# Where the lo half of a weight tile is computed: GpSimd subtraction, or ScalarE negation and an accumulating DMA

## Chip, core and metric

One core of a Trainium2 chip runs the whole kernel. The metric is the device time of one execution in microseconds; lower is better. The engines named here are TensorE (PE in the profile; its weight loads are PEld), VectorE (DVE), ScalarE (ACT), GpSimd (POOL) and SyncE (SP), which here only issues DMAs. A letter q behind an engine's name means its queue, not the engine's datapath.

## What is computed

One layer of a decoder trunk on 256 tokens of width 2048, in float32. Cut to what matters here:

```
x <- LN(alpha*x + 0.5*SwiGLU_1(x))
x <- LN(alpha*x + W_out concat[GatedDeltaNet | HGRN2 | S5 | RG-LRU](split(x W_in)))
x <- LN(alpha*x + 0.5*SwiGLU_2(x))
x <- LN(alpha*x + (p W_p) * sigmoid(x W_g))

swiglu(x, wi, wo):  gate, up = split(x @ wi);  (silu(gate) * up) @ wo      # 2048 -> 2 x 5632 -> 2048
layer_norm(x, g, b): (x - mean) * rsqrt(var + 1e-5) * g + b
```

The weights of the two SwiGLU blocks, of the mixer's two projections and of the embedding gate are read once each, 684 tiles of 128 x 1024 float32 in all.

## The kernel before

Every large product is made three times on float32r operands, so that it keeps float32 accuracy: x and the weights are each split into a high part (the value rounded to float32r) and a low part (the rest), and `mm3` (line 138) adds hi*hi, hi*lo and lo*hi into one PSUM bank.

The weights come as a stream of tiles in the order of use (`wq`). `load_w` (line 106) issues one load of 512 KB from SyncE's queue into a raw tile wr. `pump` (line 115) then makes two tiles from it: wh, by a cast on ScalarE (line 126), and wl = wr - wh, by a subtraction (line 128) on VectorE, or on GpSimd when `pool_mod` is set and the tile's number is a multiple of it. `get` (line 132) hands the next pair to the products and pumps the tiles behind it; `budget` says how many split and how many raw tiles are kept ahead (2 to 8 split ones).

All of wr, wh, wl, and also x, its transposed halves xh and xl, the hidden halves hh and hl, the gains g and biases b, live in one pool of 43 slots of 128 x 1024 words. A tile's slot goes to a later tile in program order, and the first writer of the later tile waits until the last reader of the earlier one is done. The schedule is manual: each engine runs its instructions in the order in which the program issues them.

`pool_mod` is 2 (every second lo tile on GpSimd) in the last six groups of a down projection, in the mixer, in the first of the eleven column blocks of the second SwiGLU and in the embedding's product up to its last group, 1 (every one) in the last group of a SwiGLU's down projection and of the mixer's output projection, from where it holds until the layer norm behind it is done, and 0 in the rest of the SwiGLU blocks.

At the end of such a projection (`down`, line 322; `out_proj`, line 1412) the first token half T=0 is finished before T=1. `evac` (line 163) adds the result to x and takes its statistics, and `ln_gen` (line 169) is a generator whose steps are put between the products of T=1 and those of the next block: a pow of one column on GpSimd (line 175), two steps of VectorE per quarter of x (lines 181 and 182), and `xt_piece` (line 231), which transposes a quarter on TensorE (line 236), casts it on ScalarE to xh (line 238) and subtracts on VectorE to xl (line 239). TensorE's instructions for it stand in the middle of the products. The four or five tiles of the next block that are split ahead are issued before these steps.

Of the kernel before, what the change touches and what calls it, by code (L numbers as in the profile page):

```python
# [20 lines left out]
LN_EPS = 1e-5  # L21
RMS_EPS = 1e-6
NSLOT = 43
RAMP = (0, 0, 1, 2, 4)  # weight tiles split ahead of the first products


class Build:
# [57 lines left out]
        self.cnt[key] = self.cnt.get(key, 0) + 1  # L85

    def tick(self, part=None):
        """one step of every running generator, or (part 0 or 1) of every other one."""
        for g in list(self.bg):
            if part is not None and self.side.setdefault(id(g), len(self.side) % 2) != part:  # L90
                continue
            try:
                next(g)
            except StopIteration:
                self.bg.remove(g)
                self.done.append(g)
# [3 lines left out]
            self.tick()  # L100

    def budget(self, split, raw):
        """weight tiles kept ready ahead of the products: split ones, and raw ones behind them."""
        self.n_split, self.n_raw = split, raw

    def load_w(self, n):
# [8 lines left out]
    def pump(self):  # L115
        nc = self.nc
        n = len(self.wq)
        es, ed = min(self.pg + self.n_split, n), min(self.pg + self.n_split + self.n_raw, n)
        while self.pd < ed or self.ps < es:
            if self.pd < ed:  # L120
                self.load_w(1)
            if self.ps < min(es, self.pd):
                r = self.raw.pop(self.ps)
                hi = self.slot((1024,), F32R, "wh")
                lo = self.slot((1024,), F32R, "wl")
                nc.scalar.copy(out=hi, in_=r)  # L126
                eng = nc.gpsimd if self.pool_mod and self.ps % self.pool_mod == 0 else nc.vector
                eng.tensor_tensor(out=lo, in0=r, in1=hi.bitcast(F32), op=ALU.subtract)  # L128
                self.hilo[self.ps] = (hi, lo)
                self.ps += 1  # L130

# [188 lines left out]
        self.down(KF, self.hT, [2], [4], i * 2)  # L320

    def down(self, K, lhs, first, last, li, final=False, evac=None):
        """x <- LN(alpha*x + lhs @ W), W streamed as [128, 2048] rows."""
        gs = self.groups(K, first, last)
        ps = [None, None]
        st = [self.work(24, "st") for _ in range(2)]
        k0 = 0
        gb = None
        for gi, gn in enumerate(gs):
            end = k0 + gn == K  # L330
            if gi == len(gs) - 10:
                gb = self.load_gb(li)
                self.budget(*((6, 2) if final else (8, 3)))
                if li == 0:
                    self.beta_dec()
            if gi == len(gs) - 6:
                self.pool_mod = 2
            if end:
                self.drain()
                if final:  # L340
                    self.pool_mod = 0
                else:
                    self.pool_mod = 1
                    self.budget(5, 2)
                    self.new_xt()
            wt = []
            for T in range(2):
                if k0 == 0:
                    if T:
                        self.drain() if K == KF else None  # L350
                    ps[T] = [self.bank() for _ in range(4)]
                if not end:
                    for kk in range(gn):
                        if T == 0:
                            wt += [self.get(), self.get()]
                        xhi, xlo = lhs(T, k0 + kk)
                        for n in range(4):
                            whi, wlo = wt[2 * kk + n // 2]
                            s = slice((n % 2) * 512, (n % 2) * 512 + 512)
                            self.mm3(ps[T][n], xhi, xlo, whi[:, s], wlo[:, s], k0 + kk == 0, False)  # L360
                        self.tick()
                else:
                    for n in range(4):
                        for kk in range(gn):
                            if T == 0 and n % 2 == 0:
                                wt.append(self.get())
                            xhi, xlo = lhs(T, k0 + kk)
                            whi, wlo = wt[kk + gn * (n // 2)]
                            s = slice((n % 2) * 512, (n % 2) * 512 + 512)
                            self.mm3(ps[T][n], xhi, xlo, whi[:, s], wlo[:, s], k0 + kk == 0, kk == gn - 1)  # L370
                            if kk == 1:
                                self.tick()
                        (evac or self.evac)(T, n, ps[T][n], st[T])
                        self.tick()
                    self.bg.append(self.ln_gen(T, st[T], gb, final))
                    self.tick()
            k0 += gn

# [1 line left out]
    def small(self, shape, name="m"):  # L380
        n = 1
        for d in shape:
# [25 lines left out]
        self.nc.scalar.activation(out=out, in_=a, func=f, **kw)  # L408

    def load_xt(self):  # L410
        """transposed x and the first weights, in the order in which they are used."""
        nc = self.nc
        self.new_xt()
        src = self.a["xT"].rearrange("(n c p) t -> p n c t", n=4, p=128)
# [32 lines left out]
            for h in range(2):  # L447
                self.nc.gpsimd.dma_start(out=self.x[T][h], in_=self.a["x"][0, T * 128:(T + 1) * 128, h * 1024:(h + 1) * 1024])

# [1 line left out]
    def load_params(self):  # L451
        nc, a = self.nc, self.a
        nc.gpsimd.dma_start(out=self.ident, in_=a["cst"][:, 0:128])
# [12 lines left out]
        return self.chp[:, i:i + 4]  # L466

    def softplus(self, x, n):
        """log(1 + e^x) = max(x, 0) + 2 atanh(e / (2 + e)), e = exp(-|x|), for small tiles."""
        W = lambda: self.small((n,), "sp")  # L470
        e, s, s2, q, mx = W(), W(), W(), W(), W()
        self.act(e, x, AF.Abs)
# [49 lines left out]
        self.act(self.eA, self.row[:, 0:4], AF.Exp)  # L522
        yield

# [1 line left out]
    def s5_prep(self):  # L526
        nc, a = self.nc, self.a
        S = lambda *sh: self.small(sh, "s5")
# [39 lines left out]
        yield  # L568

        def sincos(cs, sn, hs, m, n, ph):  # L570
            """cos, sin and sin^2(half) of m * (rh + rl); m, n, ph like cs."""
            sh = [128, cs.shape[1], 16] if cs.shape[2] == 16 else [128, 16, cs.shape[2]]
            if cs.shape[2] == 16:
                bh, bl = (v[:, None, :].to_broadcast(sh) for v in (rh, rl))
# [75 lines left out]
        Bre, Bim, Cre, Cim = (BC.rearrange("p (q g d) -> p q g d", q=4, g=16)[:, i] for i in range(4))  # L650

        def cmul(o_re, o_im, ar_, ai_, br_, bi_, q, neg_im=False):
            """complex product over the groups q; o_re and o_im get (rows, lhs, rhs, op) calls."""
            k = q.stop - q.start
            bc = lambda v: v[:, q, None].to_broadcast([128, k, 16])
            a1, a2 = u1[:, 0:k], u2[:, 0:k]
# [91 lines left out]
        return t  # L748

    def split_to(self, src, hi, lo):  # L750
        """src (f32, SBUF or PSUM) -> exact pair of float32r tiles."""
        self.nc.scalar.copy(out=hi, in_=src)
        self.sub(lo, src, hi.bitcast(F32))

    def rms_cm(self, y, gcol, key):
        """rms norm over 512 channels on the partitions, y [128, 4, 256] -> hi/lo."""
        nc = self.nc
        sq = self.slot((4, 256), F32, "sq")
        self.act(sq, y, AF.Square)
# [108 lines left out]
        yield  # L868
        yield from self.rms_cm(z, 84, "c")

# [1 line left out]
    def tail(self, o, T, key):  # L872
        """o [128 tokens, 4 heads, 128] in PSUM -> rms norm * gate, transposed into self.y[key]."""
        nc = self.nc
        sq = self.t2(4)
        ss = self.work(4, "ss", bufs=4)
# [21 lines left out]
        self.y[key] = (self.slot((4, 256), F32R, "yh"), self.slot((4, 256), F32R, "yl"))  # L898

    def gate_in(self, T, ps, gz, norm):  # L900
        """gz[:, T] = silu(ps) * norm gain (per head)."""
        z = gz[:, T].rearrange("p (a b) -> p a b", a=4)
        self.act(z, ps, AF.Silu)
        self.mul(z, z, norm[:, None, :].to_broadcast([128, 4, 128]), self.nc.gpsimd)

# [1 line left out]
    def hgrn_f(self, ps):  # L907
        F, K = self.slot((4, 256), F32, "F"), self.slot((4, 256), F32, "K")
        self.hF, self.hK = F, K
# [84 lines left out]
            yield  # L994
            yield

# [1 line left out]
    def conv(self, ps, acc, w, bias=None):  # L998
        nc = self.nc
        pad = self.W.tile([128, 4, 260], F32, tag="pad", name=self.nm("pad"))  # L1000
# [10 lines left out]
            if c % 2:  # L1011
                yield

# [1 line left out]
    def gdn_bd(self, ps):  # L1015
        """beta, decay logits -> per-token gates and the decay matrices."""
        nc = self.nc
        bd = self.slot((256,), F32, "bd")[0:16]
        nc.scalar.copy(out=bd, in_=ps)
# [42 lines left out]
        self.flags.add("D")  # L1062

    def tok(self, src, n):
        """token-major copy in PSUM of chunk n of channel-major src."""
        ps = self.bank((4, 128), "tok")
        for h in range(4):
            self.nc.tensor.transpose(ps[:, h], src[:, h, n * 128:(n + 1) * 128], self.ident)
# [13 lines left out]
        return ss[:, :, None].to_broadcast([128, 4, 128])  # L1082

    def tr_to(self, src, dst, neg=False):
        """dst <- per-head transpose of src [128, 4, 128]."""
        ps = self.bank((4, 128), "trt")
        for h in range(4):
            self.nc.tensor.transpose(ps[:, h], src[:, h], self.ident)  # L1088
# [64 lines left out]
        self.bg.append(self.gdn_inv(1))  # L1153

    def gdn_inv(self, n):
        """Q = transpose of (I + A)^-1, by doubling blocks along the diagonal."""
        nc = self.nc
        AT = self.AT[:, n]
        TQ = self.slot((2, 4, 128), F32, "TQ")
# [86 lines left out]
            nc.tensor.matmul(po[:, h], lhsT=self.qk[:, 1, h], rhs=uh[:, 1, h], start=False, stop=True)  # L1246
        yield from self.tail(po, 1, "a")

# [1 line left out]
    def lru_x(self, ps):  # L1250
        nc = self.nc
        wab = self.slot((8, 128), F32, "wab")
# [40 lines left out]
        yield  # L1293
        yield from self.rms_cm(y, 88, "d")

# [1 line left out]
    CHUNKS = (("t", 3080, "bi"), ("c", 4104, "cu"), ("c", 512, "ak"), ("c", 0, "aq"), ("c", 2568, "bf"), ("c", 1024, "av"),  # L1297
              ("c", 2056, "bq"), ("c", 4616, "dx"), ("c", 5128, "dg"), ("t", 3592, "bg"), ("t", 1536, "az"))
    ORDER = (("c", 1024), ("d", 1536), ("b", 512), ("a", 0))
# [155 lines left out]
    def busy(self, key):  # L1455
        return self.cnt.get(key, 0) < {"a": 2, "b": 2, "c": 1, "d": 1}[key]

# [1 line left out]
    def q_ple(self):  # L1459
        w, g = self.a["ple_w"][0], self.a["ple_gate_w"][0]  # L1460
        for half in range(2):
# [61 lines left out]


def _pack(inputs):
    """Layout of the inputs for the chip: transposed, concatenated, zero-padded; nothing is computed."""
    import numpy as np

    f = np.float32
# [67 lines left out]
```

## Time and profile before

| what | value |
|---|---|
| median of 3 runs | 2131.03 us (2126.71 to 2131.29) |
| span of the profiled execution | 2125.8 us; no separate time is given for it, the three runs lie 0.9 to 5.5 us above its span |
| instructions | 25931 |
| busy: PE, DVE, ACT, POOL | 2048.0, 1175.5, 889.6, 388.9 us |
| mean granted clock of TensorE | 0.983 |

The profile is one execution on the chip. A row of a timeline gives the start and the duration in us, the engine, the line of the kernel, the operation, the tile written and the tiles read, and in brackets the idle time of the engine before it and what ended it. Several like instructions in a row are merged: x4 behind a row and the time from the first start to the last end. A "wl<-wr,wh" is the subtraction, a "wh<-wr" the cast.

### The profile page before, as it was taken

To read this page: it belongs to the slowest core of one execution; us is meant where nothing else is said; L and a number is where in the kernel's file an instruction comes from. 1 tells how busy PE (TensorE), PEld (TensorE's weight loads), DVE (VectorE), ACT (ScalarE), POOL (GpSimd) and SP (SyncE) were. 2 spreads that over 40 slices of the span, in tenths; PEclk is the share of its full clock that TensorE was granted. 3 is DMA by queue.
4 is the path that set the end of the run, shared out by engine and by line. 5 is a ranking of instruction groups with operands and counts; after the bars stand their busy time and mean duration, and the time that the engine had idled before them with its cause. 6 is when DMAs were issued, how large, how long until landed. Compare 5 with 4: busy or idle time off the path is not lost.

```text
span 2125.8 us, 25931 instructions
## 1 busy us (share of the span) xinstructions
PE 2048.0 (96%) x10168; PEld 1731.5 (81%) x10168; DVE 1175.5 (55%) x1348; ACT 889.6 (42%) x1044; POOL 388.9 (18%) x225
## 2 busy tenths in 40 slices
PE   8999999999999989889998989999999999999896
PEld 6888788888888869889996868888888888888785
DVE  6677754445454365666466666444454455444635
ACT  5543433344443324653353524333444444434351
POOL 0000100000000443233226852000000000002453
PEclk9999999999999999899999999999999999999998
DMA  9555755656666546333335735555555566666371
GB/s 332 185 192 189 241 195 180 202 172 209 217 219 231 185 139 214 132 110 120 105 125 176 246 122 188 190 188 170 180 177 180 179 207 207 218 231 224 101 253 54
DMA packets 166058, 392.41 MB, mean 185 GB/s; under 512 B 12144, under 2 KB 14192, under 8 KB 165936
## 3 DMA queue, kind: packets, MB, share of 16 engines
q1 hardware_dynamic: 157968, 362.59, 51.7%
q0 software_dynamic: 5520, 19.52, 2.6%
q10 hardware_dynamic: 2448, 8.65, 1.2%
q8 instruction: 79, 1.29, 0.2%
q14 instruction: 43, 0.35, 0.1%
HBM read 381.80 MB, written 8.91 MB: 184 GB/s over the span
## 4 chain that ended last, share of the span: by engine, by line
PE 48%; DVE 4%; issue 2%; ACT 1%; POOL 0%; DVEq 0%; POOLq 0%; ACTq 0%
PE ps L140 14%; PE ps L141 14%; PE ps L142 14%; PE ps L1346 1%; PE ps L1347 1%; PE ps L1348 1%; DVE x L182 1%; DVE x L181 1%; PE pl L952 1%; PE p L1189 0%; DVE t L390 0%; PE hT L278 0%; PE p L1184 0%; ACT L408 0%; PE trt L1088 0%
## 5 line engine op out<-in xcount | busy, mean ns | idle before, releaser
L128 DVE TENSOR_TENSOR wl<-wr,wh 128x1024 fp32r<-128x1024 f32 x570 | 737.2, 1306 | 503.1 <-ACT wh L126 329.2
L126 ACT CAST wh<-wr 128x1024 fp32r<-128x1024 f32 x684 | 701.4, 1051 | 575.1 <-DVE wl L128 230.7
L140 PE MATMUL ps<-wh,xh 128*128 128x512 f32 x1632 | 646.3, 396 | 7.8 <-ACT wh L126 7.8
L141 PE MATMUL ps<-wl,xh 128*128 128x512 f32 x1632 | 640.4, 392 | 4.4 <-DVE wl L128 3.7
L142 PE MATMUL ps<-wh,xl 128*128 128x512 f32 x1632 | 639.3, 392 | 0.0
L128 POOL TENSOR_TENSOR wl<-wr,wh 128x1024 fp32r<-128x1024 f32 x114 | 302.2, 2662 | 839.7 <-ACT wh L126 819.7
L140 PEld LDWEIGHTS ps<-wh,xh 128*128 128x128 f32 x1632 | 309.1, 189 | 71.6 <-ACT wh L126 8.3
L141 PEld LDWEIGHTS ps<-wl,xh 128*128 128x128 f32 x1632 | 309.0, 189 | 68.4 <-DVE wl L128 5.3
L142 PEld LDWEIGHTS ps<-wh,xl 128*128 128x128 f32 x1632 | 309.0, 189 | 65.5
L140 PE MATMUL ps<-wh,hh 128*128 128x512 f32 x704 | 274.7, 390 | 0.0
L142 PE MATMUL ps<-wh,hl 128*128 128x512 f32 x704 | 274.0, 389 | 0.0
L141 PE MATMUL ps<-wl,hh 128*128 128x512 f32 x704 | 273.9, 389 | 0.0
L142 PEld LDWEIGHTS ps<-wh,hl 128*128 128x128 f32 x704 | 132.1, 188 | 27.7
L141 PEld LDWEIGHTS ps<-wl,hh 128*128 128x128 f32 x704 | 132.2, 188 | 27.2
L140 PEld LDWEIGHTS ps<-wh,hh 128*128 128x128 f32 x704 | 132.1, 188 | 27.1
L1346 PE MATMUL ps<-xh,wh 128*128 128x256 f32 x512 | 153.5, 300 | 0.0
L1347 PE MATMUL ps<-xl,wh 128*128 128x256 f32 x512 | 146.9, 287 | 0.0
L1348 PE MATMUL ps<-xh,wl 128*128 128x256 f32 x512 | 146.8, 287 | 0.0
L273 DVE SCALAR_TENSOR_TENSOR t<-t,ps 128x512 f32<-128x512 f32 x44 | 30.1, 684 | 157.9 <-PE ps L142 156.7
L271 ACT ACTIVATE t<-ps 128x512 f32<-128x512 f32 x44 | 26.3, 598 | 183.9 <-PE ps L142 183.9
L1347 PEld LDWEIGHTS ps<-xl,wh 128*128 128x128 f32 x512 | 100.5, 196 | 0.2
L1346 PEld LDWEIGHTS ps<-xh,wh 128*128 128x128 f32 x512 | 100.4, 196 | 0.2
(323 smaller groups left out, 1409.6 us busy)
## 6 DMA issues: line engine op xcount, KB each, us to landing
wr<-in_ffn_wi SPq DMA_DIRECT2D x352, 512.0 KB, 3.9
wr<-in_ffn_wo SPq DMA_DIRECT2D x176, 512.0 KB, 4.4
wr<-in_mix_w_in SPq DMA_DIRECT2D x88, 512.0 KB, 3.5
wr<-in_mix_w_out SPq DMA_DIRECT2D x32, 512.0 KB, 4.7
wr<-in_ple_gate_w SPq DMA_DIRECT2D x32, 512.0 KB, 4.7
s5l<-s5tab POOLq DMA_DIRECT2D x13, 512.0 KB, 7.0
g<-in_ln_g ACTq DMA_DIRECT2D x8, 512.0 KB, 6.2
b<-in_ln_b ACTq DMA_DIRECT2D x8, 512.0 KB, 7.5
```

The lines of the kernel that those rows point to most:

```text
L126: nc.scalar.copy(out=hi, in_=r)
L128: eng.tensor_tensor(out=lo, in0=r, in1=hi.bitcast(F32), op=ALU.subtract)
L140: mm(ps, lhsT=xhi, rhs=whi, start=first, stop=False)
L141: mm(ps, lhsT=xhi, rhs=wlo, start=False, stop=False)
L142: mm(ps, lhsT=xlo, rhs=whi, start=False, stop=last)
L181: nc.vector.scalar_tensor_tensor(out=xs, in0=xs, scalar=mv[:, 0:1], in1=g[n // 2][:, sl], op0=ALU.subtract, op1=ALU.mult)
L182: nc.vector.scalar_tensor_tensor(out=xs, in0=xs, scalar=rs[:, 1:2], in1=b[n // 2][:, sl], op0=ALU.mult, op1=ALU.add)
L271: nc.scalar.activation(out=sil, in_=pg, func=AF.Silu)
L273: nc.vector.scalar_tensor_tensor(out=h, in0=sil, scalar=0.5, in1=pu, op0=ALU.mult, op1=ALU.mult)
L1346: mm(o, lhsT=whi[:, s, cs], rhs=xhi, start=k == 0 and c % 2 == 0, stop=False)
L1347: mm(o, lhsT=whi[:, s, cs], rhs=xlo, start=False, stop=False)
L1348: mm(o, lhsT=wlo[:, s, cs], rhs=xhi, start=False, stop=k == 15 and c % 2 == 1)
```

## The change

When `pool_mod` selects a tile, GpSimd no longer subtracts. ScalarE writes the negated raw tile into wl, which is a float32r tile and so takes the negated high part, and a DMA issued from GpSimd's queue adds the raw tile to it. The tiles of VectorE stay as they are. The rest of the change takes comments and docstrings out.

```diff
@@ pump
                 hi = self.slot((1024,), F32R, "wh")
                 lo = self.slot((1024,), F32R, "wl")
                 nc.scalar.copy(out=hi, in_=r)
-                eng = nc.gpsimd if self.pool_mod and self.ps % self.pool_mod == 0 else nc.vector
-                eng.tensor_tensor(out=lo, in0=r, in1=hi.bitcast(F32), op=ALU.subtract)
+                if self.pool_mod and self.ps % self.pool_mod == 0:
+                    nc.scalar.mul(out=lo, in_=r, mul=-1.0)
+                    nc.gpsimd.dma_start(out=lo, in_=r, accum_op=ALU.add)
+                else:
+                    nc.vector.tensor_tensor(out=lo, in0=r, in1=hi.bitcast(F32), op=ALU.subtract)
                 self.hilo[self.ps] = (hi, lo)
                 self.ps += 1
```

## Rows read from the trace of the kernel before

**Rows 1.** The page's first part: busy time, share of the span and instructions of TensorE.

```profile
PE 2048.0 (96%) x10168; PEld 1731.5 (81%) x10168; DVE 1175.5 (55%) x1348; ACT 889.6 (42%) x1044; POOL 388.9 (18%) x225
```

**Rows 2.** The page's costliest groups: the cast on ScalarE and the subtraction on GpSimd. Columns: count, busy us, mean ns of one, idle time before them and what ended most of it.

```profile
L126 ACT CAST wh<-wr 128x1024 fp32r<-128x1024 f32 x684 | 701.4, 1051 | 575.1 <-DVE wl L128 230.7
...
L128 POOL TENSOR_TENSOR wl<-wr,wh 128x1024 fp32r<-128x1024 f32 x114 | 302.2, 2662 | 839.7 <-ACT wh L126 819.7
```

**Rows 3.** Busy time by stretches of 25 us: start and end, length, then PE, PEld, DVE, ACT and POOL busy us (instructions), TensorE's granted clock, the share of the DMA engines' time, GB/s.

```profile
750.00:775.00 25.00, 19.55 (x91) 15.63 (x90) 24.20 (x28) 9.20 (x12) 12.41 (x6) 0.94 0.46 147
775.00:800.00 25.00, 21.97 (x104) 16.91 (x104) 8.58 (x7) 4.24 (x6) 12.13 (x12) 0.85 0.53 196
...
2025.00:2050.00 25.00, 25.00 (x112) 20.71 (x111) 11.28 (x7) 12.72 (x13) 15.88 (x7) 1.00 0.86 296
```

**Rows 4.** VectorE's timeline in the second handover: the first and the last of six long steps of the layer norm of T=1, and the step after them.

```profile
1258.57 2.85 DVE L182 SCALAR_TENSOR_TENSOR x<-x,rs,b 128x512 f32<-128x512 f32 x1 [0.45 <-POOL rs L175]
...
1273.02 2.27 DVE L181 SCALAR_TENSOR_TENSOR x<-x,mv,g 128x512 f32<-128x512 f32 x1
1275.32 0.75 DVE L182 SCALAR_TENSOR_TENSOR x<-x,rs,b 128x512 f32<-128x512 f32 x1
```

**Rows 5.** Waits from 1240 to 1300 us, then from 1985 to 2030 us: TensorE's transposes waiting for VectorE; us in total, times, longest us.

```profile
PE xtp L236 <- DVE x L182: 8.5, 4, 3.6
...
PE xtp L236 <- DVE x L182: 5.8, 3, 2.2
```

**Rows 6.** GpSimd's timeline in the first handover: the last of five subtractions ahead, the pow of T=0, and the train of subtractions behind the pow of T=1.

```profile
739.71 2.39 POOL L128 TENSOR_TENSOR wl<-wr,wh 128x1024 fp32r<-128x1024 f32 x1 [1.16 <-ACT wh L126]
748.35 1.02 POOL L175 TENSOR_TENSOR rs<-rs,nhalf 128x1 f32<-128x1 f32 x1 [6.24 <-DVE rs L174]
...
763.55 16.21 POOL L128 TENSOR_TENSOR wl<-wr,wh 128x1024 fp32r<-128x1024 f32 x6
```

**Rows 7.** ScalarE's timeline in the first handover: the casts of the chain (the four of 727.93 to 738.59 by their first and last), and the four casts between the last xh cast of T=0 and the first of T=1.

```profile
712.14 1.05 ACT L126 CAST wh<-wr 128x1024 fp32r<-128x1024 f32 x1 [2.80 <-PE ps L141]
...
715.70 1.06 ACT L126 CAST wh<-wr 128x1024 fp32r<-128x1024 f32 x1 [1.15 <-POOL wl L128]
...
724.38 1.06 ACT L126 CAST wh<-wr 128x1024 fp32r<-128x1024 f32 x1 [0.30 <-PE ps L141]
727.93 1.05 ACT L126 CAST wh<-wr 128x1024 fp32r<-128x1024 f32 x1 [2.50 <-POOL wl L128]
...
738.59 1.05 ACT L126 CAST wh<-wr 128x1024 fp32r<-128x1024 f32 x1 [2.50 <-POOL wl L128]
...
759.63 3.90 ACT L126 CAST wh<-wr 128x1024 fp32r<-128x1024 f32 x4
```

**Rows 8.** ScalarE's timeline in the mixer: an activation of a whole 128x1024 tile.

```profile
1111.61 1.06 ACT L408 ACTIVATE gi<-gi 128x1024 f32<-128x1024 f32 x1
```

**Rows 9.** GpSimd's timeline at the mixer's start: seven issues of a plain DMA, one behind the other.

```profile
788.56 3.84 POOL L747 DMA_DIRECT2D s5l<-s5tab  x7
```

**Rows 10.** DMA issues of GpSimd's queue by stretch, 257 to 264 us, 893 to 901 us and 787 to 805 us (two rows): count, KB each, median us from issue to landing.

```profile
s5tab<-tt POOLq DMA_DIRECT2D x1, 512.0 KB, 3.5
...
gw<-in_s_glu_w POOLq DMA_DIRECT2D x2, 512.0 KB, 4.5
...
s5l<-s5tab POOLq DMA_DIRECT2D x7, 512.0 KB, 9.8
msk<-in_cst POOLq DMA_DIRECT2D x2, 512.0 KB, 4.3
```

**Rows 11.** One stretch of the table of stretches, columns as in rows 3, while those seven DMAs and the loads of weights are in flight.

```profile
793.00:803.00 10.00, 10.00 (x74) 8.60 (x73) 0.00 (x0) 2.82 (x4) 0.00 (x0) 1.00 1.03 406
```

**Rows 12.** The page's DMA issues: loads of weights for the mixer and for the embedding.

```profile
wr<-in_mix_w_in SPq DMA_DIRECT2D x88, 512.0 KB, 3.5
...
wr<-in_ple_w SPq DMA_DIRECT2D x4, 512.0 KB, 4.2
```

**Rows 13.** ScalarE's timeline in the third handover: the first and the last cast of the chain.

```profile
1952.91 1.05 ACT L126 CAST wh<-wr 128x1024 fp32r<-128x1024 f32 x1 [2.80 <-PE ps L141]
...
1979.36 1.05 ACT L126 CAST wh<-wr 128x1024 fp32r<-128x1024 f32 x1 [2.50 <-POOL wl L128]
```

**Rows 14.** GpSimd's timeline in the third handover: the pow of T=0.

```profile
1989.12 1.01 POOL L175 TENSOR_TENSOR rs<-rs,nhalf 128x1 f32<-128x1 f32 x1 [6.24 <-DVE rs L174]
```

**Rows 15.** ScalarE's timeline in the second handover: the casts of the chain.

```profile
1213.92 1.06 ACT L126 CAST wh<-wr 128x1024 fp32r<-128x1024 f32 x1 [1.67 <-PE ps L141]
1218.15 1.05 ACT L126 CAST wh<-wr 128x1024 fp32r<-128x1024 f32 x1 [3.18 <-DMA wr<-in_mix_w_out]
1221.70 2.00 ACT L126 CAST wh<-wr 128x1024 fp32r<-128x1024 f32 x2 [2.50 <-POOL wl L128]
1227.61 1.05 ACT L126 CAST wh<-wr 128x1024 fp32r<-128x1024 f32 x1 [3.91 <-POOL wl L128]
...
1234.72 1.05 ACT L126 CAST wh<-wr 128x1024 fp32r<-128x1024 f32 x1 [2.51 <-POOL wl L128]
```

**Rows 16.** GpSimd's timeline in the second handover: the pow of T=0.

```profile
1243.32 0.99 POOL L175 TENSOR_TENSOR rs<-rs,nhalf 128x1 f32<-128x1 f32 x1 [5.08 <-DVE rs L174]
```

**Rows 17.** TensorE's timeline in the mixer: a product that waited for a lo tile of GpSimd.

```profile
1118.74 0.50 PE L141 MATMUL ps<-wl,xh 128*128 128x512 f32 x1 [0.72 <-POOL wl L128]
```

## The prediction

> **What bounds the kernel now.** I read the busy table first: TensorE is busy for 96% of the span, so only the places where it stops can be won or lost [rows 1]. The list of groups gives the size of what is changed: GpSimd makes 114 of the 684 lo tiles at 2.66 us each, 302 us of an engine that has room, and ScalarE's cast in front of each costs 1.05 us [rows 2]. The table of stretches shows where TensorE stops: the mixer, and the three handovers where a layer norm feeds the next product, which I call A (about 750 us), B (1250) and C (2000). In A's two stretches TensorE is busy 19.55 and 21.97 of 25 us and VectorE 24.20 in the first, so VectorE is what ends last there [rows 3]. The timeline of VectorE in B says why: six steps of the norm (lines 181 and 182) take 2.25 to 2.88 us while GpSimd runs its train of subtractions, and the same step takes 0.75 us as soon as that has paused [rows 4]. TensorE's transposes wait 8.5 us for line 182 there and 5.8 us in C [rows 5]. Without GpSimd's reads of SBUF this loss should shrink. That is what speaks for the change.
>
> The timeline of GpSimd in A holds what speaks against it. After the last of five subtractions comes the pow of line 175, on the same in-order queue; it starts at 748.35 us, the moment its input is there [rows 6]. The tile x that it completes goes into the first transpose at line 236, which TensorE's queue holds in the middle of the last products. A pow that comes late therefore stops TensorE for the whole delay. ScalarE's timeline shows that those five tiles form a chain: each cast starts when the subtraction before it has ended, because the raw tile that it read is the next hi tile's slot [rows 7]. A step of it takes 3.55 us now.
>
> **The change, part by part.** Write L for the time from the issue of one accumulating DMA to its landing.
>
> *Removed:* 114 subtractions on GpSimd, and with them the lock between the two engines. Six steps of the norm at about 2.6 us become about 0.75: some 11 us of VectorE per handover [rows 4]. TensorE can get back no more than it waits: 8.5 us in B, about as much in A, 5.8 in C, 22.8 together [rows 5]. I take 15 (6, 6 and 3), because between the fourth xh cast and the first xh cast of the second half stand four casts [rows 7], which become eight instructions (8.2 us in place of 3.9) and become the next bound; and because the first lo tiles of the new product, issued behind the second pow, land only L later.
>
> *Added on ScalarE:* one 128x1024 instruction per tile. The row of an activation of this shape has 1.06 us [rows 8]. 114 of them are 121 us on an engine that is 42% busy; outside the chains they are hidden by the tiles' lead over the products. In the chains they count in full: a cast and a negation are 2.1 us, with the semaphore to GpSimd 2.2.
>
> *Added on GpSimd:* an issue, 0.55 us by seven issues in 3.84 us [rows 9]. The queue holds it until the negation is done, and pow, memsets and plain loads stand behind it.
>
> *L.* No accumulating DMA is in this trace. The nearest rows are plain 512 KB transfers of the GpSimd queue: one alone lands in 3.5 us, pairs in 4.3 and 4.5, and one of a train of seven in 9.8 in the median [rows 10]. The accumulate must read its destination as well; 512 KB more at the 406 GB/s of the busiest stretch [rows 11] is 1.3 us. So L is 4.4 + 1.3 = 5.7 us; I take it because the chain's DMAs go one by one, as the pairs nearly do. The ends are 3.5 (the destination's read costs nothing) and 9.8.
>
> *Moved: the release of the raw tile.* It now waits for the landing. A step of the chain becomes 2.2 + L = 7.9 us in place of 3.55.
>
> Handover A. The cast at 712.14 starts it; the next cast (715.70) takes that raw slot: 714.3 + L. Its own raw slot goes to a load on SyncE: 716.5 + 2L, and the load lands 3.5 us later [rows 12], at 720.0 + 2L. That is the tile cast at 724.38 now. Four more steps of 2.2 + L lead to the last cast, 728.8 + 6L; its pair, the semaphore and the issue (2.75) let the pow start at 731.6 + 6L = 765.8 us in place of 748.35: 17.5 us late.
>
> Handover C has the same casts, from 1952.91 to 1979.36, with its pow at 1989.12 [rows 13, 14]: the same sum, with a load of 4.2 in place of 3.5 us: 18.2 us late.
>
> Handover B. From the cast at 1213.92 five steps follow, one of them with two pairs [rows 15]: 1213.92 + 5 x (2.2 + L) + 2.1 + 2.75 = 1258.3 us, in place of a pow at 1243.32 [rows 16]: 14.9 us late. I keep the first cast where it is; if the chain before it slips, 2 to 3 us come on top.
>
> *Mixer and the end.* In the mixer VectorE steps get cheaper, against some 45 negations in ScalarE's queue and one lo tile that TensorE took with no slack at 1118.74 [rows 17]. It could be 8 us either way; I take 0. In the last product loads already keep the DMA engines 86% busy [rows 3], and a read-modify-write beside every second load may slow them: 0 to 10 us, taken at 0. Elsewhere the lead hides L: the budget keeps 3 to 8 split tiles ahead of the products, and twelve products of a tile take 2.7 us at the 112 in 25 us of a full stretch [rows 3]. The lower granted clock after a stop (0.94 and 0.85 in A's stretches [rows 3]) is paid today already; I take no more of it, with 5 us per handover as the bound.
>
> *Sum:* 17.5 + 18.2 + 14.9 - 15 = +35.6 us. Every microsecond of L is worth 6 + 6 + 5 = 17 us. The profiled execution has a span of 2125.8 us; the runs are 0.9 to 5.5 us above it, their median 2131.03. On that median: 2167 us.
>
> **The rivals.**
> *The landing is as quick as a plain copy, and the relief wins.* At L = 3.5 the three delays are 50.6 - 17 x 2.2 = 13.2 us, the relief is nearer 20, and the time is 2124 us; with the full 22.8 us of relief and the mixer's 8 us it is 2113. For it: VectorE's rows are plain, and the chain rests on the least certain number. Against it: 3.5 us is a transfer with nothing beside it, without the second read. The turning point is L of about 4: above it the kernel is slower. The Trainium skill (DMA: Bandwidth & Descriptors, Anatomy of one DMA) gives a DMA of the GpSimd queue 2.0 us plus its bytes at 436 GB/s, by which an estimate for 512 KB is 3.2 us, and the sum by it would be 2119 us, this rival's case; the rows of plain copies here, 3.5 to 4.5 us, are all longer.
> *The accumulate is slow in itself.* At L = 9.8 the delays are 50.6 + 17 x 4.1 = 120 us and the time is 2131 + 120 - 15 = 2236 us. For it: nothing here shows the speed of arithmetic in a transfer, and loads share the engines. Against it: the chains lie where loads are few.
> *It cancels.* At L near 4, delays of about 21 us meet a relief of about 20: 2127 to 2135 us.
>
> **How the numbers follow.** A difference of about 0.2%, 4 us, is what a measurement of this kernel can tell from none. Forecast (L from 4.2 to 7.5, 2136 to 2198 us): 0.49. Slow accumulate: 0.25. Quick landing: 0.18. Cancelled: 0.08. So faster 0.18, same 0.08, slower 0.74. The range goes from 2116, most of the quick case, to 2240, the slow one at the longest row: it leaves out the ends of both. The forecast's own range is 2136 to 2198.
>
> **What would show it.** The steps of ScalarE's casts before each pow are 7 to 9 us apart and wait for a DMA; line 175's first pow in A starts near 766 us, and TensorE stands still in front of the first transpose for 15 to 20 us in each of A, B and C. Lines 181 and 182 all take about 0.75 us. If the casts stay 3.55 to 5 us apart, L or the slots were misjudged. If lines 181 and 182 still take over 2 us, the relief was. If TensorE waits for lo tiles in the long products, the lead that I counted on isn't there.

## The result

| | kernel before | kernel after |
|---|---|---|
| median device time | 2128.87 us (2126.17 to 2131.29) | 2145.87 us (2139.64 to 2147.00) |
| ratio after / before | | 1.0078, 95% interval 1.0060 to 1.0096 |
| profiled execution: time, span | span 2125.8 us | 2139.64 us, span 2137.7 us |

The change costs 17 us, 0.8%. The forecast was an increase of 36 us, for a reason that turns out to be nearly absent: the direction was right, the size less than half, and the way there wrong. The profiled execution of after is the shortest of its four (the others took 2145.8 to 2147.0 us), so its trace holds some 6 us less than the median.

The page of after, first its busy times, which answer to [rows 1], then the groups and the DMA issues that the change touches, which answer to [rows 2]. Line numbers are three higher below the edit: L144 is the hi*lo product of `mm3`, L1351 its like in the mixer, L131 VectorE's subtraction, L128 the negation, L129 the DMA issue, L178 the pow, L184 and L185 the two steps of the norm, L239 the transposes.

```profile
PE 2043.4 (96%) x10168; PEld 1726.1 (81%) x10168; DVE 1055.2 (49%) x1348; ACT 995.3 (47%) x1158; POOL 186.3 (9%) x225
...
q0 software_dynamic: 21936, 79.30, 17.5%
...
L131 DVE TENSOR_TENSOR wl<-wr,wh 128x1024 fp32r<-128x1024 f32 x570 | 692.4, 1226 | 647.1 <-ACT wh L126 481.4
...
L144 PE MATMUL ps<-wl,xh 128*128 128x512 f32 x1632 | 640.2, 392 | 26.7 <-DMA wl<-wr 25.1
...
wl<-wr POOLq DMA_DIRECT2D x114, 512.0 KB, 7.9
```

VectorE and GpSimd are less busy by 120 and 203 us, ScalarE more by 106. An accumulating DMA lands 7.9 us after its issue in the median, where 5.7 was forecast. And TensorE now waits for a releaser that before did not exist: the landing of wl. Its table of waits, over the whole span (us in total, times, longest):

```profile
PE ps L144 <- DMA wl<-wr: 35.7, 14, 8.7
...
PE xtp L239 <- DVE x L185: 12.3, 7, 2.7
...
PE ps L1351 <- DMA wl<-wr: 9.2, 2, 6.1
```

Lo tiles that have not landed cost TensorE 35.7 + 9.2 = 44.9 us. The transposes' wait for the norm, 18.8 us in the same table of before, is 12.3. The stretches of 25 us show where; the first two answer to the first two of [rows 3], and [rows 3] has the stretch from 2025 too.

```profile
750.00:775.00 25.00, 20.71 (x102) 16.02 (x100) 19.87 (x31) 14.45 (x19) 6.92 (x8) 1.00 0.87 222
775.00:800.00 25.00, 24.89 (x159) 21.76 (x160) 3.91 (x5) 10.61 (x16) 6.55 (x11) 1.00 1.04 293
800.00:825.00 25.00, 18.87 (x143) 18.67 (x143) 5.50 (x13) 8.75 (x12) 2.64 (x3) 0.86 1.00 315
...
1200.00:1225.00 25.00, 20.31 (x87) 15.72 (x85) 2.77 (x4) 11.49 (x13) 5.17 (x6) 1.00 1.05 295
1225.00:1250.00 25.00, 18.47 (x62) 14.26 (x63) 11.19 (x19) 7.70 (x9) 4.04 (x5) 0.73 0.99 258
1250.00:1275.00 25.00, 22.38 (x110) 18.08 (x109) 15.18 (x24) 18.55 (x23) 7.01 (x8) 1.00 0.95 225
...
2000.00:2025.00 25.00, 14.79 (x70) 11.47 (x68) 7.95 (x10) 14.80 (x21) 3.78 (x5) 0.93 1.03 268
2025.00:2050.00 25.00, 22.20 (x90) 18.25 (x91) 4.90 (x4) 10.12 (x10) 2.59 (x3) 0.87 0.77 186
...
2075.00:2100.00 25.00, 17.14 (x67) 13.09 (x67) 4.50 (x4) 9.81 (x11) 2.59 (x3) 0.86 0.76 191
```

The same stretches of before, from 800, 1200 and 2075, have no hole:

```profile
800.00:825.00 25.00, 25.00 (x209) 24.85 (x208) 10.99 (x15) 10.90 (x16) 8.38 (x3) 1.00 0.66 226
...
1200.00:1225.00 25.00, 25.00 (x112) 20.71 (x111) 6.61 (x3) 9.44 (x10) 20.69 (x8) 1.00 0.82 287
...
2075.00:2100.00 25.00, 25.00 (x112) 20.67 (x111) 8.99 (x14) 4.79 (x7) 3.91 (x3) 1.00 0.01 2
```

In handover A (750 to 800) TensorE does more than before. It has new holes at the mixer's start (800), in the output projection (1200 to 1250) and in the embedding's product (2000 to 2100), and in each of them the DMA engines are busy for 0.76 to 1.05 of the time. They move less for it: 186 GB/s at 0.77 from 2025, where before moved 296 at 0.86, and 295 at 1.05 from 1200, where before moved 287 at 0.82.

The timelines show both sides. VectorE in handover B, the norm of T=1, beside [rows 4]:

```profile
1263.04 0.74 DVE L184 SCALAR_TENSOR_TENSOR x<-x,mv,g 128x512 f32<-128x512 f32 x1
1263.82 0.75 DVE L185 SCALAR_TENSOR_TENSOR x<-x,rs,b 128x512 f32<-128x512 f32 x1
```

All its steps take 0.74 or 0.75 us; the long ones of before are gone. The Trainium skill (SBUF — State Buffer, Who interferes with whom) says that a VectorE instruction with two SBUF inputs contends with a GpSimd instruction that reads SBUF, and that DMA does not contend with engines. The trace agrees on both counts: 0.75 us here with the DMA engines 0.95 busy, against 2.25 to 2.88 beside GpSimd's subtractions.

GpSimd and ScalarE in handover A, beside [rows 6, 7]: the last two DMA issues ahead of the pow of T=0 and that pow, then the instructions ahead of it on ScalarE that the view puts down to the landing of such a DMA.

```profile
748.54 0.86 POOL L129 DMA_DIRECT2D wl<-wr  x1 [5.80 <-ACT wl L128]
750.44 0.86 POOL L129 DMA_DIRECT2D wl<-wr  x1 [1.04 <-ACT wl L128]
751.09 0.90 POOL L178 TENSOR_TENSOR rs<-rs,nhalf 128x1 f32<-128x1 f32 x1
```

```profile
726.36 1.05 ACT L126 CAST wh<-wr 128x1024 fp32r<-128x1024 f32 x1 [4.34 <-DMA wl<-wr]
...
730.24 1.06 ACT L128 ACTIVATE wl<-wr 128x1024 fp32r<-128x1024 f32 x1 [0.49 <-DMA wl<-wr]
...
740.53 1.06 ACT L128 ACTIVATE wl<-wr 128x1024 fp32r<-128x1024 f32 x1 [3.11 <-DMA wl<-wr]
...
746.24 1.05 ACT L126 CAST wh<-wr 128x1024 fp32r<-128x1024 f32 x1 [4.65 <-DMA wl<-wr]
```

The chain of six steps is not there. ScalarE waits five times for a landing, 0.5 to 5.9 us (the fifth, ahead of a cast at 715.77, is listed as "issue" and ends when the DMA issued at 709.26 lands), and two tiles are under way at a time. What is left of the chain is its end: the pow at 751.09 stands behind the issue at 750.44, though its input was there at 748.15.

```profile
748.00 0.15 DVE L177 TENSOR_SCALAR rs<-mv 128x1 f32<-128x1 f32 x1
```

It starts 2.9 us after its input, where the pow of before starts 0.1 us after. In B and C it is 2.9 and 2.7 us, by the same two timelines, and the first transposes behind the three pows wait 2.5, 2.4 and 2.3 us; 17.5, 14.9 and 18.2 were forecast. What TensorE does wait for looks like this, its timeline at the start of the embedding's product:

```profile
2018.67 0.39 PE L143 MATMUL ps<-wh,xh 128*128 128x512 f32 x1
2027.80 0.79 PE L144 MATMUL ps<-wl,xh 128*128 128x512 f32 x1 [8.75 <-DMA wl<-wr]
...
2028.82 0.63 PE L143 MATMUL ps<-wh,xh 128*128 128x512 f32 x1
2029.24 0.63 PE L144 MATMUL ps<-wl,xh 128*128 128x512 f32 x1
```

The hi*hi product is done, the hi*lo product behind it stands 8.75 us for its tile. The stop costs more than that: up to 2031.38 the products start some 0.43 us apart, ahead of the stop 0.23, which is 1.8 us for eight of them. The granted clock from 2027 to 2032 is 0.54, most of it at 1.2 GHz.

### The profile page after: what moved, and what is told of

It reads as the page before. It is cut to its first block, busy times and chain, and to the rows that moved or that the text cites. A ratio compares the mean times of both kernels' runs of the same rounds, so it can differ in the third digit from the quotient of the medians.

```text
span 2137.7 us, 26145 instructions
## 1 busy us (share of the span) xinstructions
PE 2043.4 (96%) x10168; PEld 1726.1 (81%) x10168; DVE 1055.2 (49%) x1348; ACT 995.3 (47%) x1158; POOL 186.3 (9%) x225
## 3 DMA queue, kind: packets, MB, share of 16 engines
q0 software_dynamic: 21936, 79.30, 17.5%
## 4 chain that ended last, share of the span: by engine, by line
PE 68%; DMA 10%; issue 8%; ACT 3%; DVE 3%; POOL 1%; SPq 0%; POOLq 0%; ACTq 0%; DVEq 0%
PE ps L144 19%; PE ps L145 19%; PE ps L143 19%; DMA wl<-wr 7%; PE ps L1349 2%; PE ps L1351 2%; PE ps L1350 2%; DMA wr<-in_mix_w_out 1%; ACT wh L126 1%; DMA wr<-in_ffn_wi 1%; PE hT L281 1%; ACT wl L128 1%; DMA s5l<-s5tab 1%; POOL wl L129 1%; PE pl L955 1%
## 5 line engine op out<-in xcount | busy, mean ns | idle before, releaser
L131 DVE TENSOR_TENSOR wl<-wr,wh 128x1024 fp32r<-128x1024 f32 x570 | 692.4, 1226 | 647.1 <-ACT wh L126 481.4
L144 PE MATMUL ps<-wl,xh 128*128 128x512 f32 x1632 | 640.2, 392 | 26.7 <-DMA wl<-wr 25.1
L145 PE MATMUL ps<-wh,xl 128*128 128x512 f32 x1632 | 638.7, 391 | 0.0
L144 PEld LDWEIGHTS ps<-wl,xh 128*128 128x128 f32 x1632 | 308.7, 189 | 93.8 <-DMA wl<-wr 29.0
L145 PEld LDWEIGHTS ps<-wh,xl 128*128 128x128 f32 x1632 | 308.3, 189 | 64.6
L145 PE MATMUL ps<-wh,hl 128*128 128x512 f32 x704 | 274.6, 390 | 0.0
L144 PE MATMUL ps<-wl,hh 128*128 128x512 f32 x704 | 274.5, 390 | 0.0
L129 POOL DMA_DIRECT2D wl<-wr x114 | 98.8, 869 | 1088.4 <-ACT wl L128 1028.3
L1351 PE MATMUL ps<-xh,wl 128*128 128x256 f32 x512 | 147.1, 287 | 9.2 <-DMA wl<-wr 9.2
L145 PEld LDWEIGHTS ps<-wh,hl 128*128 128x128 f32 x704 | 132.5, 188 | 27.9
L144 PEld LDWEIGHTS ps<-wl,hh 128*128 128x128 f32 x704 | 132.6, 188 | 27.4
L128 ACT ACTIVATE wl<-wr 128x1024 fp32r<-128x1024 f32 x114 | 120.8, 1059 | 40.1 <-DMA wl<-wr 31.6
L1351 PEld LDWEIGHTS ps<-xh,wl 128*128 128x128 f32 x512 | 99.8, 195 | 9.6 <-DMA wl<-wr 9.6
## 6 DMA issues: line engine op xcount, KB each, us to landing
s5l<-s5tab POOLq DMA_DIRECT2D x13, 512.0 KB, 14.3
```

The lines of the kernel that those rows point to most:

```text
L128: nc.scalar.mul(out=lo, in_=r, mul=-1.0)
L129: nc.gpsimd.dma_start(out=lo, in_=r, accum_op=ALU.add)
L131: nc.vector.tensor_tensor(out=lo, in0=r, in1=hi.bitcast(F32), op=ALU.subtract)
L144: mm(ps, lhsT=xhi, rhs=wlo, start=False, stop=False)
L145: mm(ps, lhsT=xlo, rhs=whi, start=False, stop=last)
L1351: mm(o, lhsT=wlo[:, s, cs], rhs=xhi, start=False, stop=k == 15 and c % 2 == 1)
```

## The experiments

The theory after the result: (T) taking GpSimd's subtractions away gains some 30 us, and lo tiles that land late take back more, since the accumulating DMAs share busy DMA engines with the weight loads. Rivals: ScalarE's negations cost it; the addition is slow by itself; the loads are slowed, not the lo tiles; or the forecast's chains are at work after all. Where the time went is read from markers: the start of the pow of T=0 (A, B, C and, in the last norm, D), and the copy of the mixer's first result (hv). All are starts in the timelines of the profiled executions, in us:

| kernel | A | hv | B | C | D | span |
|---|---|---|---|---|---|---|
| before | 748.3 | 795.0 | 1243.3 | 1989.1 | 2100.1 | 2125.8 |
| after | 751.1 | 786.7 | 1241.6 | 1981.1 | 2111.3 | 2137.7 |
| plain copy | 749.4 | 785.1 | 1211.3 | 1948.3 | 2063.8 | 2091.3 |
| lo not read | 748.2 | 783.9 | 1220.5 | 1957.8 | 2069.1 | 2095.4 |
| all on VectorE | 749.1 | 788.7 | 1228.9 | 1968.9 | 2078.3 | 2104.6 |
| DMA late | 749.2 | 788.3 | 1247.8 | 1987.0 | 2117.9 | 2144.1 |
| DMA early | 750.8 | 786.3 | 1230.7 | 1970.9 | 2078.7 | 2104.9 |
| DMA in the mixer | 749.5 | 789.6 | 1222.6 | 1962.8 | 2070.6 | 2096.8 |
| mixer and A | 747.5 | 783.2 | 1218.8 | 1958.8 | 2066.6 | 2094.1 |
| change, old slots | 767.8 | 807.7 | 1294.3 | 2053.1 | 2195.4 | 2221.7 |

**1. The DMA by itself.** A kernel that does nothing but this:

```diff
+        def seq(kind, n):
+            for i in range(n):
+                if kind == "acc":
+                    nc.gpsimd.dma_start(out=lo, in_=r, accum_op=ALU.add)
+                else:
+                    nc.gpsimd.dma_start(out=lo, in_=r)
+                nc.scalar.mul(out=lo, in_=r, mul=-1.0)
...
+        seq("acc", 6)
+        seq("copy", 6)
+        gate()        # the loads below wait for the lines above
+        loads(96)
+        seq("acc", 10)
+        seq("copy", 10)
```

> Leaves out the whole layer: it only moves one 512 KB tile from SBUF to SBUF by the GpSimd queue, one transfer at a time, six accumulating and six plain ones with nothing beside them, then ten and ten beside a stream of 512 KB weight loads. Theory (the lo tiles land late because they share the DMA engines with the weight loads): alone about 4.5 us from issue to landing for the accumulating and 3.5 us for the plain one, beside the loads 8 to 11 and 6 to 9 us. Rival (the addition in the transfer is slow by itself): the accumulating one takes 7 us or more alone, and the plain one stays near 3.5 to 5 beside the loads.

The DMA view by stretch: accumulating alone (0 to 41 us), plain alone (41 to 66), accumulating beside loads (82 to 181), plain beside loads (181 to 243). Of each, the queue's packets, MB and share of 16 engines, and the issues with their median time to landing:

```profile
q0 software_dynamic: 864, 3.15, 40.5%
lo<-r POOLq DMA_DIRECT2D x6, 512.0 KB, 4.5
...
q0 software_dynamic: 864, 3.15, 34.7%
lo<-r POOLq DMA_DIRECT2D x6, 512.0 KB, 2.9
...
lo<-r POOLq DMA_DIRECT2D x9, 512.0 KB, 9.6
...
lo<-r POOLq DMA_DIRECT2D x7, 512.0 KB, 7.4
```

Alone, 4.5 against 2.9 us; beside loads, 9.6 against 7.4. Both causes are there: the addition costs 1.6 us in quiet, and company costs 4.5 to 5.1 more, whichever kind it is. The share says what the addition does to others: for the same 3.15 MB it holds the engines 0.405 x 41 = 16.6 us, the copy 0.347 x 25 = 8.7 us, half as long. The Trainium skill's figure for a DMA of the GpSimd queue (DMA: Bandwidth & Descriptors, Anatomy of one DMA), by which the prediction estimated 3.2 us, agrees with the plain copy alone, 2.9 us; none of the other three stretches comes near it.

**2. The transfer without the addition.**

```diff
-                    nc.gpsimd.dma_start(out=lo, in_=r, accum_op=ALU.add)
+                    nc.gpsimd.dma_start(out=lo, in_=r)
```

> Leaves out the subtraction: the DMA copies the raw tile into the lo tile instead of adding it; all instructions, waits and slots stay. Theory (the traffic beside the loads makes it late): landings fall from a median of 7.9 to about 6.5 us, TensorE still waits for lo tiles in the out-projection and the embedding's product, and the time is 2133 to 2142 us. Rival (the accumulate is slow in itself): landings of 4 to 4.5 us, and some 30 us of relief come out with little against them: 2105 to 2120 us.

2091.62 us, ratio to before 0.9827 (0.9812 to 0.9841): 38 us faster than before, 54 faster than the change. The landing, and TensorE's wait for it:

```profile
wl<-wr POOLq DMA_DIRECT2D x114, 512.0 KB, 5.6
```

```profile
PE ps L144 <- DMA wl<-wr: 7.3, 3, 3.4
```

So the time lies outside both sides of the expectation: the landing is still late, 5.6 us, but 2.3 us less of it empty TensorE's waits from 44.9 to 7.3 us. The tiles were only just late. No slots are moved in this comparison: built, the two programs have all 2254 tiles of the pool in the same slots. The spans of the two profiled executions are 46.4 us apart. Of these, 37.6 are waits for lo tiles, 3.9 waits for the norm (12.3 and 8.4), and 7.7 busy time (2043.4 and 2035.7), in which the slow products behind a stop are. For slower weight loads nothing is left: TensorE's waits for casts, which late loads would lengthen, are 7.7 and 7.8 us. It is also the prediction's own L (5.7 us) put to the test, and at that L the kernel gains 38 us instead of losing 36.

**3. The negation alone.**

```diff
                     nc.scalar.mul(out=lo, in_=r, mul=-1.0)
-                    nc.gpsimd.dma_start(out=lo, in_=r, accum_op=ALU.add)
+                    nc.gpsimd.tensor_tensor(out=lo, in0=r, in1=hi.bitcast(F32), op=ALU.subtract)
```

> ScalarE writes the negated tile as in the change, and GpSimd subtracts as before, behind it. Theory (ScalarE's negations are hidden): 2127 to 2135 us, beside some 2129 of the kernel before. Rival (the longer pairs of ScalarE delay the chain ahead of the pow, five or six times 1.06 us in each of three handovers, and casts of the mixer): 2140 to 2150 us.

2129.01 us, ratio 1.0002 (0.9994 to 1.0011). ScalarE's 121 us are hidden, in the handovers too.

**4. No helper at all.**

```diff
-                if self.pool_mod and self.ps % self.pool_mod == 0:
-                    nc.scalar.mul(out=lo, in_=r, mul=-1.0)
-                    nc.gpsimd.dma_start(out=lo, in_=r, accum_op=ALU.add)
+                if False:
+                    pass
                 else:
                     nc.vector.tensor_tensor(out=lo, in0=r, in1=hi.bitcast(F32), op=ALU.subtract)
```

> No GpSimd subtraction and no DMA: VectorE makes all lo tiles. Theory (the change gains some 30 us by keeping GpSimd out of VectorE's way, and loses them and more by late lo tiles): the gain in the mixer, about 16 us, stays, and in the handovers 5 or 6 more subtractions of 1.2 us each on VectorE take back about what the quicker norm steps give: 2108 to 2120 us. Rival (the gain comes from the work taken off VectorE's path by another engine, so VectorE as the handover's bound gets 6 to 8 us longer in each and the mixer too): 2135 to 2155 us.

2108.95 us, ratio 0.9903 (0.9889 to 0.9916). VectorE does 114 subtractions more and the kernel is 20 us faster than before. The groups of VectorE, every lo tile and the two steps of the norm:

```profile
L130 DVE TENSOR_TENSOR wl<-wr,wh 128x1024 fp32r<-128x1024 f32 x684 | 826.8, 1225 | 513.5 <-ACT wh L126 381.9 <-PE ps L143 116.9 <-PE ps L144 8.5
L184 DVE SCALAR_TENSOR_TENSOR x<-x,rs,b 128x512 f32<-128x512 f32 x28 | 22.8, 813 | 4.0 <-POOL rs L177 3.2
L183 DVE SCALAR_TENSOR_TENSOR x<-x,mv,g 128x512 f32<-128x512 f32 x28 | 22.1, 791 | 0.0
```

The norm's steps sum to 44.9 us; in the kernel before the same two groups are 36.1 and 38.9. GpSimd's help cost more than it gave.

**5 to 7. The DMA in one part, VectorE elsewhere.** All three add a switch, set at different places:

```diff
-                if self.pool_mod and self.ps % self.pool_mod == 0:
+                if self.lo_dma and self.pool_mod and self.ps % self.pool_mod == 0:
...
     def out_proj(self):
+        self.lo_dma = True     # late: off at the start, on from here to the end
+        self.lo_dma = False    # early: on at the start, off from here; mixer: the same, but on only from the line below
...
                 self.budget(3, 3)
                 self.pool_mod = 2
+                self.lo_dma = True     # mixer: behind the first column block
```

> DMA lo tiles only from the start of the mixer's output projection to the end; before that VectorE makes those that the DMA made. Theory (the loss lies where weight loads keep the DMA engines busy, in the output projection and the embedding's product): some 30 us on top of the 2109 us of VectorE alone, so 2130 to 2145 us. Rival (the loss is spread over all tiles, or lies in the mixer): 2112 to 2125 us.

> DMA lo tiles only up to the start of the mixer's output projection (first handover and mixer); VectorE makes the rest. Theory: what the DMA gains in the first handover, some 4 us beside VectorE alone, and in the later mixer, some 8, is partly lost at the mixer's start, where the table loads stand: 2098 to 2110 us. Rival (the loss is spread, or lies in the mixer): 2115 to 2130 us.

> DMA lo tiles only in the mixer behind its first column block, up to the output projection; VectorE makes the rest. Theory (few loads there, so the tiles land in 4.5 to 6 us, and VectorE is relieved): 2096 to 2106 us. Rival (also there the DMA is worth less than VectorE's subtraction): 2109 to 2118 us.

Late: 2146.35 us, ratio 1.0091 (1.0074 to 1.0108), 37 us more than VectorE alone. By the markers 19 of them lie between hv and B (459.5 in place of 440.2) and 21.5 between C and D (130.9 in place of 109.4); B to C is unchanged. TensorE's waits for lo tiles from 1150 to 1250 us and from 1985 to 2120 (L145 here is L144 of after):

```profile
PE ps L145 <- DMA wl<-wr: 8.7, 4, 2.9
...
PE ps L145 <- DMA wl<-wr: 16.0, 4, 7.3
```

So 8.7 of the 19 us and 16.0 of the 21.5 are direct waits. Of the rest in B, 3.7 us are the pow, which starts 3.8 us after its input, behind a DMA's issue, and the granted clock from 1150 to 1250 is 0.93, where VectorE alone has 1.00.

Early: 2107.85 us, ratio 0.9907 (0.9892 to 0.9922). A to hv takes 35.5 us in place of 39.6 (1.7 of it because the pow, where this stretch begins, starts that long after its input), but hv to B 444.4 in place of 440.2: what the handover gains, the mixer's start gives back. Mixer: 2099.77 us, ratio 0.9873 (0.9858 to 0.9888); hv to B is 433.0. So the loss is not spread over the tiles. The DMA loses in the output projection, in the embedding's product and in the mixer's first column block, where the table loads stand (s5l takes 14.3 us to land in the early kernel, 8.1 in the mixer's), and gains 2 to 4 us in A and 7 in the rest of the mixer.

**8. Nobody waits for the lo tile.**

```diff
                     nc.gpsimd.dma_start(out=lo, in_=r, accum_op=ALU.add)
+                    lo = hi
```

> The change, but TensorE multiplies by the high tile twice where the lo tile came from the DMA, so that no product waits for a landing (the lo products of 114 tiles are left out); negations, issues, traffic and slots stay. Theory (what costs is TensorE's wait for late lo tiles): 2080 to 2100 us. Rival (the transfers slow the weight loads, or hold back the raw tiles' slots): 2125 to 2145 us.

2099.80 us, ratio 0.9872 (0.9857 to 0.9887): 46 us below the change, with the same negations, issues and traffic. TensorE's wait for the norm, and the loads of mix_w_out:

```profile
PE xtp L240 <- DVE x L186: 19.8, 6, 13.0
```

```profile
wr<-in_mix_w_out SPq DMA_DIRECT2D x32, 512.0 KB, 11.5
```

The loads are no quicker in it (11.5 us to land, 7.8 in after), so slower loads are not the cause of the 46 us. That this is so near the 44.9 us which the table of waits of after puts down to the landings is partly luck. This program has 1399 tiles in other slots than the change, and the longest wait for the norm, 13.0 us, is in B: there the pow starts 13.4 us after its input, right behind a DMA's issue. That is the delay that the forecast counted on (14.9 us in B), come back with other slots. Without it experiment 8 would be some 13 us faster, an estimate from that wait.

**9 and 10. The slots.** In the kernel before, the raw slot of one tile was the next hi tile's. A tile's slot is chosen while the program is built, and in the changed program 1343 of the pool's 2254 tiles have another one. (The plain copy has the change's slots; experiments 3 to 8 and 11 have slots of their own.) So each program was built with the other's slots, written out as a list:

```diff
+SLOTS = (
+    "..."            # one letter for each of the 2254 tiles
+)
...
-        self.S = ctx.enter_context(tc.tile_pool(name="S", bufs=NSLOT))
+        self.S = ctx.enter_context(tc.tile_pool(name="S", bufs=1))
...
-        t = self.S.tile([128, 1024], dt, tag="s", name=self.nm(name))
+        t = self.S.tile([128, 1024], dt, tag=SLOTS[self.sn], name=self.nm(name))
+        self.sn += 1
```

> The change, with each tile held by hand in the slot that it has in the kernel before. Theory (the chains of casts that the prediction counted on were real with those slots, and are gone because the tiles got other slots in the changed program): the casts ahead of the first handover's pow step by some 8 us and wait for a DMA, that pow comes 15 to 25 us later than in the kernel before, and the time is 2165 to 2220 us. Rival (with the old slots too the chain has room, or is broken by the load between): 2138 to 2152 us, as the change.

> The kernel before, with each tile held by hand in the slot that it has in the changed kernel. Theory (the gain beside the change comes from GpSimd's work leaving VectorE alone, the slots by themselves are worth nothing as long as subtractions are short): 2124 to 2134 us. Rival (part of the gain in the first handover and the mixer is the slots'): 2095 to 2118 us.

The change with the old slots: 2223.11 us, ratio 1.0439 (1.0425 to 1.0453), 77 us more than the change with its own. ScalarE's timeline ahead of the pow of A, then GpSimd's, then TensorE's waits for the norm (lines are 26 further down than in after) in A (705 to 790 us), B (1275 to 1330) and C (2040 to 2090):

```profile
744.15 1.05 ACT L152 CAST wh<-wr 128x1024 fp32r<-128x1024 f32 x1 [9.97 <-DMA wl<-wr]
...
751.02 1.04 ACT L152 CAST wh<-wr 128x1024 fp32r<-128x1024 f32 x1 [4.87 <-issue]
...
757.87 1.04 ACT L152 CAST wh<-wr 128x1024 fp32r<-128x1024 f32 x1 [4.85 <-issue]
...
764.87 1.04 ACT L152 CAST wh<-wr 128x1024 fp32r<-128x1024 f32 x1 [5.00 <-DMA wl<-wr]
```

```profile
760.17 0.86 POOL L155 DMA_DIRECT2D wl<-wr  x1 [5.99 <-ACT wl L154]
767.17 0.86 POOL L155 DMA_DIRECT2D wl<-wr  x1 [6.14 <-ACT wl L154]
767.82 0.90 POOL L204 TENSOR_TENSOR rs<-rs,nhalf 128x1 f32<-128x1 f32 x1
```

```profile
PE xtp L265 <- DVE x L211: 19.7, 1, 19.7
...
PE xtp L265 <- DVE x L211: 13.1, 1, 13.1
...
PE xtp L265 <- DVE x L211: 25.5, 3, 21.2
```

Here is the prediction's chain: casts 6.9 to 7.0 us apart, each behind the landing of the DMA before (two of them appear as "issue", where the view found no releaser), a pow at 767.8 (765.8 was forecast), and TensorE standing 19.7, 13.1 and 21.2 us in A, B and C, 54 us together (17.5, 14.9 and 18.2 were forecast, 50.6 together). That A is met to 2 us is partly luck: of the last four landings of its chain one took 9.5 us and three took 4.5, 23.0 together, where four times 5.7 was counted. The lo tiles' lateness comes on top. The kernel before with the new slots: 2127.07 us, ratio 0.9993 (0.9984 to 1.0002). The slots by themselves are worth nothing while a subtraction takes 2.7 us.

**11. The best of both.** The mixer's DMA, and the DMA also in handover A:

```diff
                     self.pool_mod = 1
+                    self.lo_dma = li == 0
                     self.budget(5, 2)
...
         if T:
             self.pool_mod = 2
+            self.lo_dma = False
```

> As the kernel with the DMA in the mixer behind its first column block, and also for the tiles that are selected during the first handover up to the end of its layer norm; VectorE makes the rest. Theory (in the first handover the DMA takes VectorE's subtractions off the norm, 4 us, and the tiles beside the table loads stay on VectorE): 2094 to 2099 us. Rival (lo tiles that land late at the mixer's start, or table loads held up behind the negations, take it back): 2100 to 2108 us.

2097.11 us, ratio 0.9851 (0.9838 to 0.9864): 32 us below the kernel before and 49 below the change. Its interval overlaps that of the mixer alone, so the last 3 us are not certain; A to hv takes 35.7 us, as in the change.

## Why the prediction was wrong, step by step

**The bound and the relief.** That VectorE's long steps come from GpSimd and would fall to 0.75 us was right. The size was not: 15 us were taken, for the handovers alone. With no product waiting for a lo tile the change is worth 2099.8 - 2127.1 = -27 us, in spite of 13 us of delay in B, and with a plain copy -38, in spite of 7.3 us of waits for lo tiles. So the relief is more than twice what was taken. In the kernel with VectorE alone it is 7 us from A to hv, 8 from hv to B and 6 from B to C. The mixer, put at 0, is a large part of it: from 790 to 1150 us TensorE's waits for anything but lo tiles are 22.6 us before and 7.4 after.

**The chains, "the raw tile that it read is the next hi tile's slot": the step that failed first.** It was read correctly from the trace of before, and it does not carry over to a program that is built anew. With the old slots forced the three stalls are 54 us, against 50.6 forecast; with the program's own, the three pows start 2.7 to 2.9 us after their inputs, and the transposes behind them wait 7.2 us together. So 43 of the 50.6 us belonged to a program that was not built. How much hangs on the slots shows again in experiment 8, where another assignment brings 13.0 us back in B alone.

**L of 5.7 us.** The median is 7.9: 4.5 in quiet, some 9.6 beside loads. The rows used were plain copies, 3.5 to 9.8 us [rows 10], and their train of seven is nearest to what happened. The surcharge for the addition, 1.3 us, is measured at 1.6. In the chain of A with the old slots three of the last four landings took 4.5 us, so there 5.7 was too long.

**"Elsewhere the lead hides L", and the last product at 0: the second step that failed.** The lead hides 5.6 us nearly everywhere (7.3 us of waits) and 7.9 us not (44.9). The prediction's own bound of 0 to 10 us for the embedding's product was passed: 21.5 us in the late experiment, and the output projection, which the sum does not name, costs 19. The prediction had named the sign, TensorE waiting for lo tiles in the long products, and given it no price. The warning stood in [rows 3]: DMA engines 86% busy from 2025 us.

**ScalarE's and GpSimd's parts.** The negation at 1.06 us, hidden, was right and measured at nothing. An issue of the accumulating kind takes 0.87 us, not 0.55; nothing shows that to matter.

**The sum.** It was forecast as -15 of relief and +50.6 of chains. Between the two profiled executions, whose spans are 11.9 us apart, the tables of waits and the busy times of TensorE give +44.9 for lo tiles that land late, -10.4 at the transposes (22.7 to 12.3, with the 7.2 us that are left of the chains in it), -15.8 at the mixer's own products (23.2 to 7.4), -2.8 for lo tiles that VectorE or GpSimd makes, and -4.6 of busy time: +11.3. Experiment 8 gives the like in medians, -27 and +46, but these two add up to the change whatever it costs, so they confirm nothing. That the change came out slower, as forecast, is luck: the relief was more than twice what was taken, the chains nearly absent, and the loss lay where the sum had put 0. The rival of the slow accumulate named the right quantity, but at the wrong place, the chains.

What stays open: why the builder chose other slots, and how many microseconds in experiments 3 to 8 and 11 are owed to slots of their own. Between the plain and the accumulating DMA, and in experiments 9 and 10, the slots are held.

## What to carry to other kernels

A chain through buffer slots that is read in one trace holds only for that assignment; before it goes into a sum, ask whether the edit lets the assignment change, and give "the chain dissolves" a chance of its own. A result that moves from an engine to a DMA must be held against the lead of its reader in every stage where loads already fill the DMA engines, for there 2.3 us more of landing (5.6 and 7.9 in the median) made 45 us of waiting out of 7. And when a helper engine slows the one it helps, try the version with no helper first: here that was worth 20 us with less code.

## What the runs showed of the hardware

An accumulating SBUF-to-SBUF DMA of 512 KB holds the DMA engines 1.9 times as long as a plain one (16.6 against 8.7 us of them for six), takes 0.85 to 0.88 us to issue on GpSimd against 0.53 to 0.55, and lands in 4.5 against 2.9 us alone. Beside a stream of loads it is 9.6 against 7.4 us.
